# Products of full height in the attention and the HGRN heads of a hybrid trunk

## The chip, the cores and the metric

One Trainium2 chip, one core of it. The metric is the device time of one execution in microseconds (us); lower is better. The program is compiled once, and its times are the medians of several executions.

## What is computed

A trunk of two layers over L = 1024 + 16 positions, the first 16 being learned meta tokens. Layer 0 mixes with four HGRN heads and four attention heads side by side, layer 1 with trailing-mean pooling, and each layer ends in a squared-ReLU MLP. The change touches layer 0's mixers. Cut to that:

```python
def step(S, inp):                               # HGRN, one chunk of 64 positions
    qi, ki, vi, gi = inp
    b = jnp.cumsum(gi, axis=2)
    o_inter = jnp.einsum('bhtk,bhkv->bhtv', qi * jnp.exp(b), S)
    dec = jnp.exp(jnp.where(tri, b[:, :, :, None, :] - b[:, :, None, :, :], -jnp.inf))
    att = jnp.einsum('bhtk,bhtsk,bhsk->bhts', qi, dec, ki)
    o_intra = jnp.einsum('bhts,bhsv->bhtv', att, vi)
    b_last = b[:, :, -1:, :]
    S_new = jnp.exp(b_last[:, :, 0, :])[..., None] * S + jnp.einsum(
        'bhsk,bhsv->bhkv', ki * jnp.exp(b_last - b), vi)
    return S_new, o_inter + o_intra

def mla_mixer(...):                             # attention; a head's key: 128 own columns, 64 rope columns
    q, k = rope_tail(rmsnorm(q, qn_g), cos, sin), rope_tail(rmsnorm(k, kn_g), cos, sin)
    return block_causal_attention(q, k, v, cid)

def one_block(args):                            # 128 queries of one head, all keys
    s = jnp.einsum('bqhd,bkhd->bhqk', qblk, k) * scale
    mask = cid[None, :] <= qc[:, None]          # cid: 0 for the meta tokens, then one per 64 positions
    p = jax.nn.softmax(jnp.where(mask, s, -jnp.inf), axis=-1)
    return jnp.einsum('bhqk,bkhd->bqhd', p, v)
```

## The kernel before

Everything is float32. Where precision matters, a number is held as a high part (rounded to fp32r, a shorter float that TensorE multiplies in one pass) and a low part (the rest), and a product is three fp32r products: high by high, high by low, low by high (`mm3`, lines 156 to 158). Products of plain float32 appear in the trace as two records each. The program is one straight stream of instructions: the writer gives the order of the work, a scheduler with its own time model then sets the order on each engine, and the tile pools add the waits. So each edit can move its neighbours.

The stages, in order of time: `entry` and the first projections (to 100 us of the span); `hgrn_head` for four heads, in which the next projections fill in, then `mla_in` (100 to 355); `attention` (355 to 586); `out_proj` (586 to 680); then two MLPs with the pooling between them (680 to the end).

`attention` computes values for two heads (`values`, line 692), prepares keys and queries of a head (`head_prep`), and runs `qtile` for nine blocks of queries of each head, i = 7 down to -1. Block i has 128 queries (i = -1: the 16 meta tokens) and nk = 16 + 128 (i + 1) keys. The next head's preparation, and at the end the first products of `out_proj`, are interleaved by the scheduler. In `qtile`:

- **Scores** (line 774): the keys are cut into one to three pieces of at most 512, and each piece is a chain of five products into one bank `sc`. The fourth takes the query's rope part `qs` (high in rows 0 to 63, low in 64 to 127) against the high rope keys `ks[0]`, doubled over 128 rows; the fifth takes the high rows of `qs` alone against 64 rows of the low rope keys `ks[1]`. There are 60 chains.
- **Softmax**: DVE scales the scores and finds the maximum (778), ACT takes the exponential (783), DVE the reciprocal (785), DVE scales `p` (786). `p` has two buffers, `sc` has two banks.
- **Weighted values**: blocks of `p` are transposed on PE by a product with the identity (797), up to four to a bank `tp`; they are copied to `pts` (16 rows of meta keys on DVE, 800; the rest by an engine that the scheduler picks, 803) and multiplied with the values (806): `vm` holds those of the 16 meta tokens in rows 0 to 15, `va` those of 128 keys. There are 180 transposes and 180 value products, 36 of them with `vm`.

In `hgrn_head` the first chunk is the 16 meta tokens, and its products have 16 rows: the state from them (567, `kt` by `vm`) and their own output (583, `attM` by `vm`), each once a head. The notation `16*128` in the trace is the rows and columns of the weights that a product loads, and PEld is that load.

Of the kernel before, what the change touches and what calls it, by code (L numbers as in the profile page):

```python
# [17 lines left out]
P = 128  # L18
D = 1024
NM = 16  # L20
# [39 lines left out]
class Trunk:  # L60
# [336 lines left out]
    def mixer_in(self):  # L397
        nc, V = self.nc, self.nc.vector
        small = self.small(2, "att")
        self.att = small[:, :288].rearrange("p (c t) -> p c t", t=32)  # L400
        self.attM = small[:, 288:288 + P]
        self.attT = self.slot(13, "attT")[:, :8 * P].rearrange("p (c t) -> p c t", t=P)
        V.memset(self.attT, 0.0)
        V.memset(self.attM, 0.0)
        self.vm = self.mix.tile([P, 256], F32, name="vm", tag="vm")
        self.ms = [self.small(i, f"x{i}")[:, :BW] for i in range(2)]
        gs = [self.hgrn_head(j) for j in range(H)]
        self.mla_in()
        for j in range(H):
            for off, n in SPL0:  # L410
                s = slice(off, off + n)
                self.split(gs[j][:, s], self.uh[j][:, s], self.ul[j][:, s], V if j < 3 else nc.gpsimd)

    def hgrn_head(self, j):
        nc = self.nc
        TT, V = nc.vector.tensor_tensor, nc.vector
        f, k, q, v = (self.first[i // 2] if j == 0 and i % 2 == 0 else self.slot(4 * (j % 2) + i, x)
                      for i, x in enumerate("fkqv"))
        g = self.slot(8 + j, "g")
        v = v[:, :8 * P].rearrange("p (c v) -> p c v", v=P)  # L420
        vm = self.vm[:, (j % 2) * P:(j % 2 + 1) * P]
# [33 lines left out]
        for i, (off, n) in enumerate(SPL0):  # L455
# [7 lines left out]
            b = 0  # L463
            if i == 0:
                nc.tensor.transpose(pv3[:NM, 3], vt[:, :NM], self.ident)
                V.tensor_copy(out=vm[:NM], in_=pv3[:NM, 3])
                b = NM
            m = (n - b) // P
            for c in range(m):
                nc.tensor.transpose(pv3[:, c], vt[:, b + c * P:b + (c + 1) * P], self.ident)  # L470
            c0 = (off + b - NM) // P
# [32 lines left out]
        while n < P:  # L504
            base = 0 if n < NM else NM
            width = L - base
            if n <= 16:
                level(1 + n.bit_length() - 1, k, qa)
                if n == 16:
                    for r in range(4):  # L510
                        nc.scalar.copy(out=attT[32 * r:32 * r + 32, :, 32 * r:32 * r + 32],
                                       in_=att[32 * r:32 * r + 32, 1:])
            else:
                ps = self.bank("tp")
                ps3 = ps.rearrange("p (c t) -> p c t", t=64)
                for c in range(8):
                    for b in range(64 // n):
# [3 lines left out]
                                         start=True, stop=True, tile_position=(0, r))  # L521
# [25 lines left out]
        kt = f[:, :8 * P].rearrange("p (c v) -> p c v", v=P)  # L547
        for c0 in (0, 4):
            pk = self.bank("sc")
            pk3 = pk.rearrange("p (c v) -> p c v", v=P)  # L550
# [11 lines left out]
        for c0 in (0, 4):  # L562
            pk = self.bank("sc")
            pk3 = pk.rearrange("p (c v) -> p c v", v=P)
            for c in range(c0, c0 + 4):
                rows = NM if c == 0 else P
                nc.tensor.matmul(pk3[:, c - c0], kt[:rows, c], v[:, c - 1] if c else vm[:NM], start=True, stop=True)
            for c in range(c0, c0 + 4):
                s = k[:, c * P:(c + 1) * P]
                if c == 0:  # L570
                    V.tensor_copy(out=s, in_=pk3[:, 0])
                else:
                    V.scalar_tensor_tensor(out=s, in0=st[-1], scalar=dec[:, c - 1:c], in1=pk3[:, c - c0],
                                           op0=ALU.mult, op1=ALU.add)
                st.append(s)

        V.tensor_copy(out=self.attM[:NM, :NM], in_=att[:NM, 0, :NM])
        for b in range(3):
            po = self.bank("tp")[:, :BW].rearrange("p (c v) -> p c v", v=P)
            for i in range(3):  # L580
                c = 3 * b + i
                if c == 0:
                    nc.tensor.matmul(po[:, 0], self.attM[:NM], vm[:NM], start=True, stop=True)
                    continue
                nc.tensor.matmul(po[:, i], attT[:, c - 1], v[:, c - 1], start=True, stop=False)
                nc.tensor.matmul(po[:, i], qa[:, NM + P * (c - 1):NM + P * c], st[c], start=False, stop=True)
            sq = self.tmp()
            nc.scalar.activation(out=sq, in_=po, func=AF.Square)
            col = self.mix.tile([P, 4], F32, name="colh", tag="colh", bufs=3)
            V.tensor_reduce(out=col[:, :3], in_=sq.rearrange("p (c v) -> p c v", v=P), axis=AX.X, op=ALU.add)  # L590
            nc.scalar.activation(out=col[:, :3], in_=col[:, :3], func=AF.Sqrt, scale=1.0 / P, bias=self.eps)
            V.reciprocal(out=col[:, :3], in_=col[:, :3])
            on = self.tmp().rearrange("p (c v) -> p c v", v=P)
            TT(out=on, in0=po, in1=col[:, :3].unsqueeze(2).to_broadcast([P, 3, P]), op=ALU.mult)
            pt = self.bank("tp")
            for i in range(3):
                nc.tensor.transpose(pt[:, i * P:(i + 1) * P], on[:, i], self.ident)
            pieces = [(0, 0, NM), (P, NM, 2 * P)] if b == 0 else [(0, NM + P * (3 * b - 1), BW)]
            for c0, t, n in pieces:
                V.scalar_tensor_tensor(out=g[:, t:t + n], in0=pt[:, c0:c0 + n], scalar=self.col(C_HGN),  # L600
                                       in1=g[:, t:t + n], op0=ALU.mult, op1=ALU.mult)
# [53 lines left out]
    def attention(self):  # L655
        nc = self.nc
        row = lambda i, name: self.slot(i, name, F32R)

        kna = [row(2, "kna0"), row(3, "kna1")]
        self.v = [self.slot(i, "va")[:, :8 * P].rearrange("p (c v) -> p c v", v=P) for i in (8, 9)]  # L660
        self.vm = self.mix.tile([P, 256], F32, name="vm", tag="vm")
        self.npt = 0
        qna = [row(10, "qna0"), row(12, "qna1")]
        self.rrs = [self.slot(i, "rr") for i in (13, 7)]
        qs = [row(4, "qs0"), row(11, "qs1")]
        self.pb = [self.slot(i, "p") for i in (6, 5)]
        u6, u7 = ([self.uh[c], self.ul[c]] for c in (6, 7))

        qnb = [z[:, 0] for z in self.ckv]
        sets = [(kna, qna, qs[0]), (u7, u6, qs[1]), (kna, qna, qs[0]), (u7, qnb, qs[1])]  # L670
        self.values(0)
        hs = [self.head_prep(0, *sets[0]), self.head_prep(1, *sets[1])]
        for h in range(H):
            for i in reversed(range(-1, 8)):
                self.qtile(h, i, *sets[h], hs[h])
            if h == 1:
                self.values(1)
            if h + 2 < H:
                hs.append(self.head_prep(h + 2, *sets[h + 2]))
# [79 lines left out]
    def qtile(self, h, i, kn, qn, qs, rr):  # L759
        nc, V = self.nc, self.nc.vector  # L760
        t, rows, nk = (0, NM, NM) if i < 0 else (NM + P * i, P, NM + P * (i + 1))
        q = slice(t, t + P)
# [4 lines left out]
        for z in range(np_):  # L767
            a, b = z * step, min(nk, (z + 1) * step)
            ps = self.bank("sc")[:, :b - a]
            ks = slice(a, b)  # L770
            ops = [(qn[0][:, q], kn[0][:, ks]), (qn[0][:, q], kn[1][:, ks]), (qn[1][:, q], kn[0][:, ks]),
                   (qs[:, q], self.ks[0][:, ks]), (qs[:64, q], self.ks[1][:64, ks])]
            for m, (x, y) in enumerate(ops):
                nc.tensor.matmul(ps, x, y, start=(m == 0), stop=(m == 4))
            if b == nk and i >= 0:
                V.memset(ps[:64, b - a - 64:b - a], -1e30)

            V.tensor_tensor_reduce(out=p[:rows, a:b], in0=ps[:rows], in1=rr[0][:rows, ks], op0=ALU.mult, op1=ALU.max,
                                   scale=rr[1][:rows, 1 + i:2 + i],
                                   scalar=-3e38 if z == 0 else st[:rows, z - 1:z],  # L780
                                   accum_out=st[:rows, z:z + 1])
# [3 lines left out]
        V.reciprocal(out=st[:rows, 6:7], in_=st[:rows, 5:6])  # L785
        V.tensor_scalar(out=p[:rows, :nk], in0=p[:rows, :nk], scalar1=st[:rows, 6:7], scalar2=None, op0=ALU.mult)
        po = self.bank("tp")
        v, vm = self.v[h % 2], self.vm[:NM, (h % 2) * P:(h % 2 + 1) * P]
        last = i + 1
        for g0 in range(0, i + 2, 4):  # L790
            grp = range(g0, min(g0 + 4, i + 2))
            pt = self.bank("tp").rearrange("p (c q) -> p c q", q=P)
            sb = self.small(self.npt % 3, "pts").rearrange("p (c q) -> p c q", q=P)
            self.npt += 1
            for kt in grp:
                kr, k0 = (NM, 0) if kt == 0 else (P, NM + P * (kt - 1))
                nc.tensor.transpose(pt[:kr, kt - g0, :rows], p[:rows, k0:k0 + kr], self.ident[:rows, :rows])
            b = 0
            if g0 == 0:
                V.tensor_copy(out=sb[:NM, 0, :rows], in_=pt[:NM, 0, :rows])  # L800
                b = 1
            if len(grp) > b:
                nc.any.tensor_copy(out=sb[:, b:len(grp), :rows], in_=pt[:, b:len(grp), :rows])
            for kt in grp:
                kr = NM if kt == 0 else P
                nc.tensor.matmul(po[:, :rows], v[:, kt - 1] if kt else vm, sb[:kr, kt - g0, :rows],
                                 start=(kt == 0), stop=(kt == last))
        d = slice(t, t + rows)
        self.split(po[:, :rows], self.uh[4 + h][:, d], self.ul[4 + h][:, d])
# [555 lines left out]
```

## Time and profile before

| | us |
|---|---|
| median of 3 runs (2065.58 to 2076.06) | 2068.29 |
| profiled execution, its own time | 2067.88 |
| its span in the trace | 2066.1 |
| busy in the span: PE / PEld | 2002.0 / 1826.6 |
| busy in the span: DVE / POOL / ACT | 1441.1 / 887.7 / 880.0 |

A matmul's record has a modelled end, so the share of PE says little of its speed: the step from one product's start to the next one's is what counts. An idle stretch of an engine is put down to what ended it; "issue" is a wait for nothing that the profile shows.

### The profile page before, as it was taken

Reading aid. Unit: us, or ns where it says so; the run is one execution under the profiler, and the core shown is the slowest. Engines: PE = TensorE matmul, PEld = TensorE weight load, DVE = VectorE, ACT = ScalarE, POOL = GpSimd, SP = SyncE. Lnnn points to the kernel's source line nnn. Section 1 sums busy time; section 2 is a strip of 40 time slices with the busy share of each in tenths; the row PEclk is TensorE's granted clock in tenths of the full one; section 3 lists DMA queues with packets and bytes.
Section 4 is the critical chain, followed back from the end, with each engine's and each line's share of the span. In section 5 each row is a group of like instructions: output and inputs, shape, how many; then the busy total and the mean of one; then the engine's idle time right before and its main releaser. Section 6 shows DMA issues by size and latency. Waiting matters only on the chain. (4 is left out here: it accounts for less than half of the span.)

```text
span 2066.1 us, 37157 instructions
## 1 busy us (share of the span) xinstructions
PE 2002.0 (97%) x14440; PEld 1826.6 (88%) x14440; DVE 1441.1 (70%) x2385; ACT 880.0 (43%) x1800; POOL 887.7 (43%) x632
## 2 busy tenths in 40 slices
PE   8999999999999999999989999998999999999999
PEld 7999998888799999999989999997878887778887
DVE  7655557554454777767877767779787778888676
ACT  5232325554442544454623334466444445334331
POOL 6223223000021345454447777343454454488771
PEclk9999999999999899999999999998999999999999
DMA  4111100000031244443854340101444447653402
GB/s 149 42 33 32 42 27 30 13 11 11 27 114 32 93 139 155 152 143 140 265 179 156 121 135 19 57 26 67 148 143 143 153 147 254 211 168 128 138 21 102
DMA packets 114928, 215.20 MB, mean 104 GB/s; under 512 B 12224, under 2 KB 20672, under 8 KB 114752
## 3 DMA queue, kind: packets, MB, share of 16 engines
q1 hardware_dynamic: 114752, 212.83, 30.8%
q8 instruction: 113, 1.85, 0.4%
q14 instruction: 63, 0.52, 0.1%
HBM read 151.80 MB, written 60.99 MB: 103 GB/s over the span
## 5 line engine op out<-in xcount | busy, mean ns | idle before, releaser
L139 POOL TENSOR_TENSOR wl<-raw,wh 128x1024 fp32r<-128x1024 f32 x23 | 56.2, 2444 | 356.2 <-ACT wh L138 339.4
L138 ACT ACTIVATE A<-q 128x512 fp32r<-128x512 f32 x148 | 91.2, 621 | 213.7 <-PE sc L942 131.8
L139 POOL TENSOR_TENSOR A<-q,A 128x512 fp32r<-128x512 f32 x91 | 143.6, 1586 | 83.5 <-ACT A L138 55.9
L139 POOL TENSOR_TENSOR B<-q,B 128x512 fp32r<-128x512 f32 (+1 forms) x97 | 151.2, 1572 | 46.0 <-ACT B L138 46.0
L940 PE MATMUL tp<-B,A 128*128 128x260 f32 (+5 forms) x510 | 163.1, 320 | 7.2 <-DVE hT L1144 7.0
L156 PE MATMUL mm<-uh,wh 128*128 128x384 f32 (+1 forms) x504 | 165.1, 328 | 2.5 <-DVE z L450 2.5
L157 PE MATMUL mm<-ul,wh 128*128 128x384 f32 (+1 forms) x504 | 163.7, 325 | 0.0
L158 PE MATMUL mm<-uh,wl 128*128 128x384 f32 (+1 forms) x504 | 163.0, 324 | 0.4 <-DVE wl L139 0.4
L941 PE MATMUL tp<-B,A 128*128 128x260 f32 (+5 forms) x510 | 162.2, 318 | 0.5 <-DVE B L139 0.5
L942 PE MATMUL tp<-B,A 128*128 128x260 f32 (+5 forms) x510 | 161.6, 317 | 0.0
L139 POOL TENSOR_TENSOR r<-q,r 128x512 fp32r<-128x512 f32 x66 | 91.4, 1384 | 135.7 <-ACT r L138 135.7
L940 PE MATMUL mm<-B,A 128*128 128x260 f32 (+5 forms) x345 | 110.3, 320 | 3.5 <-ACT B L138 3.5
L940 PE MATMUL sc<-B,A 128*128 128x260 f32 (+5 forms) x345 | 110.0, 319 | 0.8 <-DVE hT L1144 0.7
L138 ACT ACTIVATE r<-q 128x512 fp32r<-128x512 f32 x131 | 81.8, 627 | 66.9 <-DVE q L985 36.5
L941 PE MATMUL mm<-B,A 128*128 128x260 f32 (+5 forms) x345 | 110.2, 319 | 0.0
L940 PEld LDWEIGHTS tp<-B,A 128*128 128x128 f32 x510 | 96.7, 190 | 15.0 <-DVE hT L1144 7.7
L942 PE MATMUL mm<-B,A 128*128 128x260 f32 (+5 forms) x345 | 109.9, 318 | 0.0
L941 PE MATMUL sc<-B,A 128*128 128x260 f32 (+5 forms) x345 | 109.6, 318 | 0.0
L942 PE MATMUL sc<-B,A 128*128 128x260 f32 (+5 forms) x345 | 109.5, 317 | 0.0
L1017 ACT ACTIVATE q<-q 128x260 f32<-128x260 f32 (+2 forms) x128 | 61.5, 484 | 103.7 <-DVE q L1016 103.3
L138 ACT ACTIVATE B<-q 128x512 fp32r<-128x512 f32 (+1 forms) x154 | 92.2, 620 | 27.4 <-PE sc L942 15.4
L941 PEld LDWEIGHTS tp<-B,A 128*128 128x128 f32 x510 | 96.5, 189 | 7.7 <-DVE B L139 0.7
(656 smaller groups left out, 7005.4 us busy)
## 6 DMA issues: line engine op xcount, KB each, us to landing
q<-in_w_dn_dram SPq DMA_DIRECT2D x88, 256.0 KB, 3.0
q<-in_w_up_dram SPq DMA_DIRECT2D x75, 256.0 KB, 2.6
q<-at SPq DMA_DIRECT2D x46, 256.0 KB, 3.3
q<-at SPq DMA_DIRECT2D x44, 260.0 KB, 3.8
raw<-in_w_in_dram SPq DMA_DIRECT2D x19, 512.0 KB, 3.5
q<-a SPq DMA_DIRECT2D x36, 256.0 KB, 3.6
a<-q SPq DMA_DIRECT2D x34, 260.0 KB, 2.9
a<-q SPq DMA_DIRECT2D x31, 256.0 KB, 2.9
```

The costliest lines, as they stand in the source:

```text
L138: self.nc.scalar.activation(out=hi, in_=src, func=AF.Copy)
L139: (eng or self.nc.vector).tensor_tensor(out=lo, in0=src, in1=hi.bitcast(F32), op=ALU.subtract)
L156: self.nc.tensor.matmul(out, wh, xh, start=(i == 0), stop=False)
L157: self.nc.tensor.matmul(out, wh, xl, start=False, stop=False)
L158: self.nc.tensor.matmul(out, wl, xh, start=False, stop=(i == n - 1))
L940: mm(ps, wh, xh, start=first and i == 0, stop=False, skip_group_check=True)
L941: mm(ps, wh, xl, start=False, stop=False, skip_group_check=True)
L942: mm(ps, wl, xh, start=False, stop=i == n - 1, skip_group_check=True)
L1017: nc.scalar.activation(out=dst[:, s], in_=dst[:, s], func=AF.Square)
```

## The change

Three edits, and the fourth that they need:

- The fifth score product takes all 128 rows of `qs` and of the low rope keys `ks[1]`. Those rows were there already (`sel` doubles the keys, and `split` works on all rows), so no instruction is added. It now also adds the query's low part by the low keys.
- All products with `vm` (HGRN 567 and 583, attention 806) take 128 rows. `vm` is set to zero first, by a MEMSET on DVE in `mixer_in` and one in `attention`; the rows of the other operand below the 16 hold old finite numbers.
- The transposes take 128 rows of `p` and 128 columns of it in each case; the first one, of the 16 meta keys, becomes one of keys 0 to 127, of which rows 16 and below meet zeros.
- With that, the copy of 16 rows is dropped, and one copy takes the whole bank.

```diff
@@ mixer_in
         self.vm = self.mix.tile([P, 256], F32, name="vm", tag="vm")
+        V.memset(self.vm, 0.0)
@@ hgrn_head
-                rows = NM if c == 0 else P
-                nc.tensor.matmul(pk3[:, c - c0], kt[:rows, c], v[:, c - 1] if c else vm[:NM], start=True, stop=True)
+                nc.tensor.matmul(pk3[:, c - c0], kt[:, c], v[:, c - 1] if c else vm, start=True, stop=True)
...
-                    nc.tensor.matmul(po[:, 0], self.attM[:NM], vm[:NM], start=True, stop=True)
+                    nc.tensor.matmul(po[:, 0], self.attM, vm, start=True, stop=True)
@@ attention
         self.vm = self.mix.tile([P, 256], F32, name="vm", tag="vm")
+        nc.vector.memset(self.vm, 0.0)
@@ qtile
             ops = [(qn[0][:, q], kn[0][:, ks]), (qn[0][:, q], kn[1][:, ks]), (qn[1][:, q], kn[0][:, ks]),
-                   (qs[:, q], self.ks[0][:, ks]), (qs[:64, q], self.ks[1][:64, ks])]
+                   (qs[:, q], self.ks[0][:, ks]), (qs[:, q], self.ks[1][:, ks])]
...
-        v, vm = self.v[h % 2], self.vm[:NM, (h % 2) * P:(h % 2 + 1) * P]
+        v, vm = self.v[h % 2], self.vm[:, (h % 2) * P:(h % 2 + 1) * P]
...
             for kt in grp:
-                kr, k0 = (NM, 0) if kt == 0 else (P, NM + P * (kt - 1))
-                nc.tensor.transpose(pt[:kr, kt - g0, :rows], p[:rows, k0:k0 + kr], self.ident[:rows, :rows])
-            b = 0
-            if g0 == 0:
-                V.tensor_copy(out=sb[:NM, 0, :rows], in_=pt[:NM, 0, :rows])
-                b = 1
-            if len(grp) > b:
-                nc.any.tensor_copy(out=sb[:, b:len(grp), :rows], in_=pt[:, b:len(grp), :rows])
+                k0 = NM + P * (kt - 1) if kt else 0
+                nc.tensor.transpose(pt[:, kt - g0], p[:, k0:k0 + P], self.ident)
+            nc.any.tensor_copy(out=sb[:, :m, :rows], in_=pt[:, :m, :rows])
             for kt in grp:
-                kr = NM if kt == 0 else P
-                nc.tensor.matmul(po[:, :rows], v[:, kt - 1] if kt else vm, sb[:kr, kt - g0, :rows],
+                nc.tensor.matmul(po[:, :rows], v[:, kt - 1] if kt else vm, sb[:, kt - g0, :rows],
                                  start=(kt == 0), stop=(kt == last))
```

The scheduler moves little outside attention: POOL's order is the same, two DMA stores change places with neighbours, and PE's order differs from row 1882 to row 2540 of 11649 and then at four places in the second MLP. Three places inside.

PE, head 1, first block (i = 7), where the first bank of transposes is followed by its value products. Before:

```order
L797 MATMUL tp<-cst,p 16x128
L797 MATMUL tp<-cst,p 128x128 x3
L806 MATMUL tp<-pts,vm 128x128
L797 MATMUL tp<-cst,p 128x128 x4
L806 MATMUL tp<-pts,va 128x128 x3
L797 MATMUL tp<-cst,p 128x128
L774 MATMUL sc<-uh 128x328
L774 MATMUL sc<-ul,uh 128x328
L774 MATMUL sc<-uh,ul 128x328
L774 MATMUL sc<-ks,qs_3928 128x328 x2
```

and now (lines are those of the changed kernel: 775 for 774, 800 for 797, 803 for 806):

```order
L800 MATMUL tp<-cst,p 128x128 x4
L775 MATMUL sc<-uh 128x328
L775 MATMUL sc<-ul,uh 128x328
L775 MATMUL sc<-uh,ul 128x328
L775 MATMUL sc<-ks,qs_3930 128x328 x2
L803 MATMUL tp<-pts,vm 128x128
L803 MATMUL tp<-pts,va 128x128 x3
L800 MATMUL tp<-cst,p 128x128 x5
```

The product with `vm` stood straight behind its transposes and now stands behind a whole score chain, and the other three value products follow it at once, without transposes between.

PE, head 3, the last blocks (i = 2 to -1), where the attention's work runs out and only a little of `out_proj` is between. Before:

```order
L797 MATMUL tp<-cst,p 128x128 x2
L806 MATMUL tp<-pts,vm 128x128
L156 MATMUL mm<-uh,wh 128x384
L806 MATMUL tp<-pts,va 128x128 x2
L157 MATMUL mm<-ul,wh 128x384
L158 MATMUL mm<-uh,wl 128x384
L797 MATMUL tp<-cst,p 16x128
L797 MATMUL tp<-cst,p 128x128
L806 MATMUL tp<-pts,vm 128x128
L797 MATMUL tp<-cst,p 16x16
L806 MATMUL tp<-pts,va 128x128
L806 MATMUL tp<-pts,vm 128x16
```

and now:

```order
L800 MATMUL tp<-cst,p 128x128 x3
L156 MATMUL mm<-uh,wh 128x384
L803 MATMUL tp<-pts,vm 128x128
L803 MATMUL tp<-pts,va 128x128 x2
L157 MATMUL mm<-ul,wh 128x384
L158 MATMUL mm<-uh,wl 128x384
L800 MATMUL tp<-cst,p 128x128 x2
L803 MATMUL tp<-pts,vm 128x128
L803 MATMUL tp<-pts,va 128x128
L800 MATMUL tp<-cst,p 128x128
L803 MATMUL tp<-pts,vm 128x16
```

One `out_proj` product moved ahead of a `vm` product, and the last transpose no longer stands between the last value products.

DVE, the end of the HGRN heads (the copies of head 3's keys `f`, line 561, before the query's scaling, 630), now:

```order
L558 COPY f<-sc 16x128
L559 COPY f<-sc 128x384
L561 COPY f<-sc 128x512
L662 MEMSET vm 128x256
L630 SCALAR_TENSOR_TENSOR z<-z,par,ss 128x384
```

The MEMSET is the new row; the four others stood there in this order before.

## Rows read from the trace of the kernel before

**Rows 1.** The page, part 1: busy us, share of the span, instructions.

```profile
PE 2002.0 (97%) x14440; PEld 1826.6 (88%) x14440; DVE 1441.1 (70%) x2385; ACT 880.0 (43%) x1800; POOL 887.7 (43%) x632
```

**Rows 2.** Busy time by stretch; after the engines PEclk, DMA share, GB/s.

```profile
355.00:586.00 231.00, 224.55 (x1426) 188.22 (x1425) 122.57 (x430) 114.24 (x285) 4.40 (x3) 1.00 0.09 29
...
680.00:693.00 13.00, 12.65 (x61) 12.56 (x60) 8.80 (x18) 5.45 (x11) 0.00 (x0) 0.51 0.12 42
```

**Rows 3.** PE's waits in 355 to 586: us in total, times, longest.

```profile
PE tp L806 <- DVE pts L800: 1.6, 4, 0.4
...
PE tp L806 <- ACT pts L803: 0.2, 1, 0.2
```

**Rows 4.** Weight loads, 355 to 586: busy us, mean ns, idle before.

```profile
L797 PEld LDWEIGHTS tp<-cst,p 128*128 128x128 f32 x144 | 17.5, 142 | 1.5
...
L774 PEld LDWEIGHTS sc<-ks,qs 128*128 128x128 f32 x60 | 11.3, 188 | 0.3 <-issue 0.2
L774 PEld LDWEIGHTS sc<-ks,qs 64*128 64x128 f32 x60 | 11.0, 183 | 11.6 <-issue 9.4
L806 PEld LDWEIGHTS tp<-pts,vm 16*128 16x128 f32 x72 | 10.5, 182 | 6.9 <-DVE pts L800 2.7 <-issue 1.5 <-DVE st L785 0.3
```

**Rows 5.** PE in order of time, a score chain: start us, us, instruction.

```profile
487.07 0.89 PE L774 MATMUL sc<-kna,qna 128*128 128x456 f32 x3
...
488.49 0.39 PE L692 MATMUL mm<-wh,ckv 128*128 128x256 f32 x1
488.72 0.28 PE L692 MATMUL mm<-wl,ckv 128*128 128x256 f32 x1
...
489.07 0.28 PE L692 MATMUL mm<-wl,ckv 128*128 128x256 f32 x1
```

**Rows 6.** PE in order of time, a product with vm.

```profile
482.60 0.39 PE L797 MATMUL tp<-cst,p 128*16 128x128 f32 x2
482.82 0.61 PE L806 MATMUL tp<-pts,va 128*128 128x128 f32 x4
483.36 0.48 PE L806 MATMUL tp<-pts,vm 16*128 16x128 f32 x2
483.78 0.49 PE L806 MATMUL tp<-pts,va 128*128 128x128 f32 x2
```

**Rows 7.** PE in order of time, what follows a product with vm.

```profile
432.96 0.94 PE L806 MATMUL tp<-pts,va 128*128 128x128 f32 x6
433.73 0.38 PE L797 MATMUL tp<-cst,p 128*16 128x128 f32 x2
```

**Rows 8.** PE in order of time, a product with vm in HGRN.

```profile
111.51 0.48 PE L583 MATMUL tp<-vm,att 16*128 16x128 f32 x2
111.93 0.39 PE L156 MATMUL mm<-uh,wh 128*128 128x272 f32 x1
112.16 0.29 PE L157 MATMUL mm<-ul,wh 128*128 128x272 f32 x1
```

**Rows 9.** Copies to pts on ACT in 355 to 586.

```profile
L803 ACT COPY pts<-tp 128x384 f32<-128x384 f32 x26 | 12.2, 472 | 10.5 <-PE tp L797 5.5 <-DVE pts L800 2.9 <-DVE st L782 1.8
...
L803 ACT COPY pts<-tp 128x512 f32<-128x512 f32 x7 | 4.1, 587 | 9.2 <-PE tp L797 9.2
```

**Rows 10.** Copies to pts on DVE in 355 to 586.

```profile
L800 DVE COPY pts<-tp 16x128 f32<-16x128 f32 x32 | 8.8, 275 | 9.5 <-PE tp L797 9.5
```

**Rows 11.** PE in order of time, head 3's last blocks.

```profile
580.64 0.49 PE L797 MATMUL tp<-cst,p 128*16 128x128 f32 x3
581.57 0.48 PE L806 MATMUL tp<-pts,vm 16*128 16x128 f32 x2 [0.44 <-DVE pts L800]
```

**Rows 12.** DVE in order of time, where the second MEMSET goes.

```profile
339.07 0.67 DVE L560 COPY f<-sc 128x512 f32<-128x512 f32 x1
340.73 0.62 DVE L630 SCALAR_TENSOR_TENSOR z<-z,par,ss 128x384 f32<-128x384 f32 x1 [0.99 <-ACT ss L185]
```

**Rows 13.** PE in the same place.

```profile
340.52 1.83 PE L567 MATMUL sc<-v,f 128*128 128x128 f32 x14
```

More of the change, by code (lines that the diff above doesn't have):

```diff
@@ L791, in qtile @@
             grp = range(g0, min(g0 + 4, i + 2))
+            m = len(grp)
             pt = self.bank("tp").rearrange("p (c q) -> p c q", q=P)
```

## The prediction

> **What bounds the kernel now.** First the busy line of the page: PE is busy for 97% of the span, DVE for 70%, ACT for 43% [rows 1]. Since a product's end is modelled, that says only that PE rarely stands still, not that it is quick. Then the stretch that the change touches most, attention from 355 to 586 us: PE 224.6 of 231 us at the full granted clock, DVE 122.6, ACT 114.2 [rows 2]. PE's waits on other engines there are seven rows, from 1.6 us down to 0.2, some 6 us in all [rows 3]. So in attention a microsecond off PE's own sequence is a microsecond off the end, as long as DVE and ACT, busy about half the time, deliver early enough.
>
> Third, PE's own sequence. The reader is to look at the idle time ahead of the weight loads: the same tile `qs` is loaded 60 times at 128 rows with 0.3 us of idle time ahead of all of them, and 60 times at 64 rows with 11.6 us, most of it put down to "issue", that is to no other engine [rows 4]. The loads of `vm` have 6.9 us ahead of 72, the transposes 1.5 us ahead of 144 [rows 4]. So something happens where the height of a product changes. Its full price stands in the steps from one start to the next.
>
> **The full-height step.** From 488.72 to 489.07 three fp32r products of 256 columns start, 0.117 us each [rows 5]; 256 columns at 2.4 GHz are 0.107, so a step is the columns plus 0.01. A weight load takes 0.19 [rows 4], longer than the step: at full height it is hidden behind the product ahead. Plain float32 records of 128 columns step by 0.11 (two from 482.60 to 482.82) [rows 6].
>
> A rule speaks against this. The Trainium skill, page "TensorE: Matmul & The Clock Gate", Part 3 (row/col tiling), says that a weight load overlaps products in flight only when its row group differs. By it a fifth product of full height would still load after the fourth, and the sum below would be near zero. The steps of 0.117 under loads of 0.19 [rows 4, 5] disagree with it for full height.
>
> **The change part by part.**
>
> The score chains. A chain of five products of 456 columns begins at 487.07, the next work at 488.49: 1.42 us. At full height it would be 5 x 0.20 = 1.00. The product behind the chain then steps by 0.23 (488.49 to 488.72) in place of 0.117, because its load came late as well: another 0.11. The chain's own first product has the same 0.11 from the switch ahead of it, which is in the 1.42 and belongs to that one. So one chain costs 0.42 - 0.11 + 0.11 = 0.42 too much [rows 5]; I take 0.40, as the step's extra of 0.01 is rounded. 52 of the 60 chains have 264 columns or more: 20.8 us. The eight of 144 and 16 columns are bound by their loads anyway, and I put 0.3 on them: 2.4. Together **23 us**. The lower bound is the idle time alone, 11.6 - 0.3 = 11.3 [rows 4]; I take the steps, since they hold the late loads too, which no idle row counts. The rows added to the fifth product cost nothing: its 128 rows stand in SBUF, and a load takes 183 ns at 64 rows and 188 at 128 [rows 4].
>
> The products with `vm` in attention. The two records take 0.42 (483.36 to 483.78) against 0.22: 0.20. The four ahead take 0.54 (482.82 to 483.36) against 0.44: 0.10 [rows 6]. The six behind take 0.77 (432.96 to 433.73) against 0.66: 0.11 [rows 7]. That is 0.4 where `vm` stands among value products, and 0.2 where it follows a score chain, whose exit already counts the rest. In the order before, 15 of the 36 follow a chain: 21 x 0.4 + 15 x 0.2 = **11 us**. Lower bound: 6.9 us of idle time, less the 2.7 + 0.3 put down to DVE [rows 4], 3.9.
>
> The eight products with `vm` in HGRN. 0.42 (111.51 to 111.93) against 0.22, and the product behind, of 272 columns, 0.23 against 0.123 [rows 8]: 8 x 0.31 = **2.5 us**, at least 1.
>
> The transposes. Two from 482.60 to 482.82 step by 0.11 although the first loads 16 columns [rows 6], so the height of the output is no switch, and full ones gain or lose nothing. The four for the meta tokens' queries grow from 16 columns to 128, at most 0.1 us each.
>
> The copies. DVE loses 36 copies, 32 of them 275 ns long [rows 10]. It was busy half the time: nothing, beyond a little slack. In return 24 copies on ACT grow from 384 to 512 columns, 472 to 587 ns [rows 9]: 2.8 us on an engine that was busy half the time. But now the first product of a bank, with `vm`, waits for the big copy instead of the small one. From the last transpose's step to its first product 0.28 (record; two end 0.39 after the first starts) - 0.11 + 0.59 + some 0.05, about 0.8 us, have to be covered [rows 6, 9]. I went through the new order of PE and laid the full-height steps on the work between: of the 60 banks, 50 have 0.8 us or more of other work there, and the missing pieces of the other ten add up to 4.7 us. Most lie at the ends of heads 1 and 3, as in the second order piece above. There PE waits already now, 0.44 us at 581.57 [rows 11], and the same count on the old order gives 6.5 us, of which the trace shows 1.6 + 0.2 as waits for copies [rows 3]: the switches were the cover for the rest. This cover goes. **I give back 3 us**; bounds 0 and 9.
>
> The MEMSETs. The first stands at the start, where DVE waits for parameters. The second is a new wait: `vm` has one buffer, so DVE stands until PE has read head 3's `vm` (the product before 340.52, whose result is out at about 340.6 [rows 13]), with the scaling at line 630 queued behind it. But that scaling starts only at 340.73, after 0.99 us of idle time [rows 12], so it is late by 0.2 to 0.3 us, and PE has value products to do meanwhile. Nothing; 0.3 us without that cover.
>
> **The sum.** 23 + 11 + 2.5 = 36.5, say 37 with HGRN's entries; less 3: 34 us. On the profiled execution, 2067.9 (span 2066.1 and 1.8 around it): 2033.9. That execution lies 0.4 under the median of the runs: **2034**. By the lower bounds, 11.3 + 3.9 + 1, the gain is 16.
>
> What is late next? Behind attention, `out_proj` and the MLPs keep their order, so the gain should pass through. A loose piece is the clock: from 680 to 693 us PE ran at 0.51 of its clock, the level of 1.2 GHz [rows 2], which costs 6.4 us, and where such stretches fall can change when everything moves by 34 us: 6 us either way.
>
> **The rivals.**
>
> *Half the gain (0.10).* The idle time goes, the late loads stay, or the softmax chain sets the pace in the last blocks of each head, where PE's cover is thin [rows 11]. For it: the switches were cover there, and PE waited in spite of them. Against it: DVE and ACT at half load [rows 2]. Gain 16: 2052.
>
> *The height is not the cause (0.05).* The idle time comes with the last place in a chain, or a full-height load behind a full-height product queues as well, and each of the 60 + 44 places costs what it did. Against it: `qs` as the fourth product has no idle time ahead of its load, and going over to `vm` from value products of the same kind costs 0.10 in the middle of an accumulation [rows 4, 6]. No gain, and the clock as it was: 2068. The Trainium skill's rule on row groups, above, would lead here.
>
> *Slower (0.05).* The big copy is on the path at each of the 60 banks, because ACT, which also runs the exponentials, comes to it late. If the new work between is no cover, 60 x 0.8 = 48 us are lost against 37 won, and 2079 results; it decides from 0.62 us a bank on. Against it: in the old order the copies of 384 had the same path, and PE waited 0.2 us for them in all [rows 3].
>
> **How the numbers follow.** The full gain has 0.80. Its own range is 2034 with 0 to 9 given back and 6 of clock: 2026 to 2046. To hold 8 in 10 it reaches slightly to the half gain: 2025 to 2048. A measurement of this kernel can tell about 0.5%, 10 us, from no change; so faster is 0.80 + 0.10 = 0.90, same 0.05, slower 0.05.
>
> **What would show it.** In the profile after, the idle time ahead of the fifth product's load should fall from 11.6 to below 1 us, five products of 456 columns should step by 0.20 each, the product behind them too, and two records of `vm` should take 0.22. The attention stretch should shrink from 231 to about 200 us, with 4 to 9 us of PE's waits in it, mostly for `pts` by ACT, at the ends of heads 1 and 3. If the stretch shrinks by half of that and PE's waits grow to 20 us, the half case holds; if idle time stays ahead of a load of 128 rows, the height was not the cause. The prediction is wrong in size above all if the late loads are not due to the switch.

## The result, and the profile after

The changed kernel takes **2039.9 us** (median of four runs, 2039.06 to 2041.79) against 2066.9 (2064.99 to 2076.06) for the kernel before on the same chip. The ratio is 0.9862, with a 95% interval of [0.9844, 0.9879]; ratios here go by all runs and not by the medians, so they differ slightly from the quotient of the two. The profiled executions have spans of 2039.0 and 2066.1, so 27.1 us are to be found in the traces. Lines move with the change: the score products are now at 775, the transposes at 800, their copy at 801, the value products at 803.

The page after, part 1, against [rows 1]. PE has as many instructions as before and is busy for the same 97%; DVE lost 36 copies. The page's shares don't show that anything happened.

```profile
PE 1974.5 (97%) x14440; PEld 1824.8 (89%) x14440; DVE 1435.6 (70%) x2349; ACT 883.4 (43%) x1806; POOL 885.9 (43%) x632
```

The attention stretch after, from 355 to 557 us, against [rows 2] (columns as there). It is 202 us long where it was 231, with the same kind of filling. The second row is new: for part of 366 to 380 us the granted clock was at its lower level, 1.2 GHz, which the kernel before did not show in attention.

```profile
355.00:557.00 202.00, 195.37 (x1406) 185.55 (x1407) 114.86 (x390) 115.31 (x286) 3.41 (x2) 0.98 0.09 29
366.00:380.00 14.00, 12.73 (x66) 12.06 (x65) 6.76 (x15) 6.34 (x15) 0.00 (x0) 0.76 0.07 20
```

The weight loads after, 355 to 557 us, against [rows 4] (busy us, mean ns, idle time before):

```profile
L800 PEld LDWEIGHTS tp<-cst,p 128*128 128x128 f32 x180 | 21.4, 142 | 1.2 <-PE mm L158 0.8 <-PE tp L803 0.2
L775 PEld LDWEIGHTS sc<-ks,qs 128*128 128x128 f32 x120 | 20.6, 189 | 0.3
...
L803 PEld LDWEIGHTS tp<-pts,vm 128*128 128x128 f32 x72 | 11.5, 189 | 3.8 <-ACT pts L801 3.4
```

`qs` is now loaded 120 times at 128 rows, and all of them together have 0.3 us of idle time ahead. The 60 loads of 64 rows had 11.6. What is left ahead of `vm` is a wait for the copy on ACT; "issue" is gone.

PE in order of time, the same place as [rows 5], one block of queries in head 2:

```profile
473.27 0.78 PE L775 MATMUL sc<-kna,qna 128*128 128x456 f32 x3
473.89 0.57 PE L775 MATMUL sc<-ks,qs 128*128 128x456 f32 x2
474.30 0.28 PE L693 MATMUL mm<-wh,ckv 128*128 128x256 f32 x1
474.42 0.28 PE L693 MATMUL mm<-wl,ckv 128*128 128x256 f32 x1
```

The chain takes 1.03 us (473.27 to 474.30) instead of 1.42, and the step behind it is 0.12 instead of 0.23. Around a `vm` product, against [rows 6, 7]:

```profile
408.29 0.38 PE L803 MATMUL tp<-pts,vm 128*128 128x128 f32 x2
408.51 0.83 PE L803 MATMUL tp<-pts,va 128*128 128x128 f32 x6
409.18 0.49 PE L800 MATMUL tp<-cst,p 128*128 128x128 f32 x3
```

Its two records take 0.22 (0.42 before) and the six behind 0.67 (0.77).

**An account of PE's steps.** The rows above are samples, so I went through every step from one product's start to the next one's, from the first score product to the last value product. A full-height step is put at the columns by 2.4 GHz plus 0.015 us, at least 0.112; what a step takes beyond that is sorted by where it stands. "Change of height" is a step into or out of a product of under 128 rows, or the one just behind; "waits" are steps over 0.25 us late; "low clock" is lateness of steps begun while the granted clock was at 1.2 GHz; "other" is the rest. A small delay beside a short product counts as "change of height", whatever its cause. Both kernels have 1364 steps there, and the full-height steps add up to 178.0 us in both. In us:

| | first score product at | attention | full height | change of height | other | waits | low clock | attention's end to the span's end |
|---|---|---|---|---|---|---|---|---|
| before | 364.7 | 220.5 | 178.0 | 31.6 | 3.4 | 7.5 | 0 | 1481.0 |
| after | 361.1 | 195.5 | 178.0 | 0 | 6.0 | 8.6 | 2.9 | 1482.4 |
| difference | -3.6 | -25.0 | 0 | -31.6 | +2.6 | +1.1 | +2.9 | +1.4 |

So 31.6 us came off, 6.6 came back inside attention, 3.6 were won ahead of it and 1.4 lost behind it. Counted in the same stretch, the kernel before has 83 separate runs of short products, so that one costs 0.38 us; the changed kernel has none.

### The profile page after: what moved, and what is told of

Read it like the earlier page. It is cut to its first block, busy times and chain, and to the rows that moved or that the text cites. A ratio compares the mean times of both kernels' runs of the same rounds, so it can differ in the third digit from the quotient of the medians.

```text
span 2039.0 us, 37138 instructions
## 1 busy us (share of the span) xinstructions
PE 1974.5 (97%) x14440; PEld 1824.8 (89%) x14440; DVE 1435.6 (70%) x2349; ACT 883.4 (43%) x1806; POOL 885.9 (43%) x632
## 5 line engine op out<-in xcount | busy, mean ns | idle before, releaser
L138 ACT ACTIVATE B<-q 128x512 fp32r<-128x512 f32 (+1 forms) x154 | 92.2, 620 | 27.1 <-PE sc L939 15.4
```

Of the source, the lines that this page charges most:

```text
L138: self.nc.scalar.activation(out=hi, in_=src, func=AF.Copy)
```

## The experiments

My theory: each place where a product of fewer than 128 rows stands among full ones costs PE some 0.4 us, and the change takes these places away. The main rival: the place in the chain, or the copies and the order, did it. The account above was made for each run; where only a size is told below, it is from the same columns.

### One part alone

The fifth score product of full height, everything else as before:

```diff
-                   (qs[:, q], self.ks[0][:, ks]), (qs[:64, q], self.ks[1][:64, ks])]
+                   (qs[:, q], self.ks[0][:, ks]), (qs[:, q], self.ks[1][:, ks])]
```

> The kernel before with one edit: the fifth score product of full height; vm, transposes and copies as before. Theory (each change of height costs PE about 0.2 us going in and out together with the late load behind it, 0.4 a chain): 60 chains give about 22 us, so about 2045 against 2067, and no idle time ahead of the fifth load. Rival (the copies and transposes brought most of the 27 us): under 5 us, 2062 or more.

Measured: 2054.7 us, ratio 0.9930 [0.9909, 0.9951]. That is 10 us above the forecast. In its trace 19.4 us of changes of height came off, and 6.2 us of low clock, 1.4 of waits and 0.9 of other delays came back.

The `vm` products of attention alone, with what they need:

```diff
+        nc.vector.memset(self.vm, 0.0)
...
-        v, vm = self.v[h % 2], self.vm[:NM, (h % 2) * P:(h % 2 + 1) * P]
+        v, vm = self.v[h % 2], self.vm[:, (h % 2) * P:(h % 2 + 1) * P]
...
+                k0 = NM + P * (kt - 1) if kt else 0
+                nc.tensor.transpose(pt[:, kt - g0], p[:, k0:k0 + P], self.ident)
+            nc.any.tensor_copy(out=sb[:, :m, :rows], in_=pt[:, :m, :rows])
...
-                nc.tensor.matmul(po[:, :rows], v[:, kt - 1] if kt else vm, sb[:kr, kt - g0, :rows],
+                nc.tensor.matmul(po[:, :rows], v[:, kt - 1] if kt else vm, sb[:, kt - g0, :rows],
```

> The kernel before with only the attention's vm edits: MEMSET, vm products of 128 rows, full transposes, one copy a bank; fifth score product at 64 rows, HGRN as before. Theory: 36 vm products at 0.2 to 0.4 us, about 11 us less 2 for waits on the larger copy: about 2058. Rival (larger copy on the path at most banks): no gain or a loss, 2067 or more.

Measured: 2058.9 us, 0.9951 [0.9936, 0.9966].

The HGRN products alone (the first MEMSET, and 567 and 583 with all rows):

```diff
+        V.memset(self.vm, 0.0)
...
+                nc.tensor.matmul(pk3[:, c - c0], kt[:, c], v[:, c - 1] if c else vm, start=True, stop=True)
...
+                    nc.tensor.matmul(po[:, 0], self.attM, vm, start=True, stop=True)
```

> The kernel before with only HGRN's edits: the first MEMSET and the eight products with vm at 128 rows. Theory: about 3 us, 2064, read in the trace as the time at which the attention's first score chain starts (364.6 us before) coming about 3 us earlier. Rival (the entry to attention moved for another reason): no change of that time.

Measured: 2068.55 us, 0.9994 [0.9982, 1.0007], so the forecast 3 us are not seen in the time.

The weight loads in attention, of the first and then of the second of these kernels (columns as above):

```profile
L774 PEld LDWEIGHTS sc<-ks,qs 128*128 128x128 f32 x120 | 20.8, 193 | 0.3
...
L806 PEld LDWEIGHTS tp<-pts,vm 16*128 16x128 f32 x72 | 10.5, 182 | 7.6 <-DVE pts L800 2.8 <-issue 2.0 <-DVE ul L139 0.5
```

```profile
L803 PEld LDWEIGHTS tp<-pts,vm 128*128 128x128 f32 x72 | 11.0, 189 | 5.1 <-ACT pts L801 2.8 <-issue 1.9 <-ACT p L784 0.2
L775 PEld LDWEIGHTS sc<-ks,qs 64*128 64x128 f32 x60 | 11.0, 183 | 12.0 <-issue 10.3
```

Each edit clears its own loads and leaves the other's as they were (7.6 against 6.9 for `vm`, 12.0 against 11.6 for the 64 rows). In the account, the first leaves 12.2 us of changes of height, so 19.4 came off; the second leaves 22.1, so 9.5 came off. Together that is 28.9, and both at once take 31.6: the missing 2.7 lie where a `vm` product follows a chain directly, so that neither edit alone makes PE's passage there one of full height. By the times, the three parts give 14.5 + 10.1 + 1.2 = 26 us (2071.36, the kernel before on that chip, by one less each ratio) against 28.5 for the whole (2066.93 in the same way), a difference well within the intervals.

In HGRN the new product is as quick as forecast, the product behind it is not. PE in order of time, the HGRN kernel, against [rows 8]:

```profile
111.57 0.49 PE L583 MATMUL tp<-vm,att 128*128 128x128 f32 x2
111.81 0.37 PE L156 MATMUL mm<-uh,wh 128*128 128x272 f32 x1
112.03 0.29 PE L157 MATMUL mm<-ul,wh 128*128 128x272 f32 x1
```

The two records take 0.24 instead of 0.42. But the step behind is still 0.22 where I had counted on 0.123. So such a place gave 0.18 us, not 0.31. The first score product starts 2.1 us earlier (362.6 against 364.7), of which eight such places are 1.4; the time's interval includes no change at all.

### Place, number and dose

The 64-row product in the second place of the chain instead of the last:

```diff
+            ops = [(qn[0][:, q], kn[0][:, ks]), (qs[:64, q], self.ks[1][:64, ks]), (qn[0][:, q], kn[1][:, ks]),
+                   (qn[1][:, q], kn[0][:, ks]), (qs[:, q], self.ks[0][:, ks])]
```

> The kernel before with the score chain's 64-row product moved from fifth to second place; same products, same result. Theory (the change of height costs, wherever it is): the same two changes a chain, time within 5 us of the kernel before, and the same 11 us of idle time ahead of the 60 loads of 64 rows. Rival (the last place in the chain costs): the idle time goes, about 2050.

Measured: 2074.28 us, 1.0018 [1.0007, 1.0029].

The fourth product with 64 rows as well, beside the fifth:

```diff
-                   (qs[:, q], self.ks[0][:, ks]), (qs[:64, q], self.ks[1][:64, ks])]
+                   (qs[:64, q], self.ks[0][:64, ks]), (qs[:64, q], self.ks[1][:64, ks])]
```

> The kernel before with the fourth score product cut to 64 rows too (it leaves out the query's low rope part), so that each chain has two products of 64 rows side by side. Theory (it is the change that costs, not the low product): one change in and one out as before, so the same time within 5 us, and next to no idle time ahead of the second of the two loads. Rival (each product of 64 rows costs): about 20 us more, 2087.

Measured: 2074.44 us, 1.0017 [0.9997, 1.0038].

The 64-row product twice, in the second place and in the last, with full products between:

```diff
+            ops = [(qn[0][:, q], kn[0][:, ks]), (qs[:64, q], self.ks[1][:64, ks]), (qn[0][:, q], kn[1][:, ks]),
+                   (qn[1][:, q], kn[0][:, ks]), (qs[:, q], self.ks[0][:, ks]), (qs[:64, q], self.ks[1][:64, ks])]
```

> The kernel before with a second copy of the 64-row product at second place of each score chain, so that each chain changes height four times instead of twice (the low rope keys are added twice, which the reference does not do). Theory: 60 more products, 19008 columns at 2.4 GHz, 8 us plus 1 of steps, and 60 more pairs of changes at the 0.32 us that undoing the chains alone showed, 19: about 28 us more, 2095. Rival (a fixed price a chain, or the queue hides a second change): 9 us more, 2076.

Measured: 2112.5 us, 1.0194 [1.0155, 1.0234].

The loads of `qs` in these three, in that order:

```profile
L774 PEld LDWEIGHTS sc<-ks,qs 128*128 128x128 f32 x60 | 11.3, 189 | 0.2
L774 PEld LDWEIGHTS sc<-ks,qs 64*128 64x128 f32 x60 | 11.0, 183 | 10.4 <-issue 8.8
```

```profile
L774 PEld LDWEIGHTS sc<-ks,qs 64*128 64x128 f32 x120 | 18.2, 189 | 11.9 <-issue 9.8
```

```profile
L774 PEld LDWEIGHTS sc<-ks,qs 64*128 64x128 f32 x120 | 22.3, 186 | 22.2 <-issue 18.1
...
L774 PEld LDWEIGHTS sc<-ks,qs 128*128 128x128 f32 x60 | 11.5, 192 | 0.4 <-issue 0.3
```

The idle time goes with the 64 rows and not with the place: 10.4 us in the second place, while the load that is now last, of 128 rows, has 0.2. With two products of 64 rows side by side there are 120 such loads and still 11.9 us, as with 60. With two apart there are 22.2. So a passage into another height and out again is what costs, and a second product of the same height in it is free. The account says the same in full size: the changes of height are 31.1 us with two side by side (31.6 before), and 53.8 with two apart, 22.2 more for 60 more passages, or 0.37 us each. In the second place they are 36.8, 5.2 more: 14 `vm` products that stood directly behind the chain's 64-row product now stand apart from it, which makes 97 runs of short products out of 83.

The kernel with two apart was 43 us slower where 28 had been forecast. The passages (22.2) and the 60 added products (9.3) explain 31.5. What is over is clock: the stretch as a whole, and the longest part of it at the lower level (columns as in the windows above).

```profile
355.00:630.00 275.00, 270.29 (x1480) 213.60 (x1479) 123.92 (x431) 115.09 (x285) 4.38 (x3) 0.94 0.09 27
363.00:384.00 21.00, 20.53 (x78) 16.69 (x77) 5.88 (x11) 5.56 (x12) 1.00 (x1) 0.60 0.00 0
```

The granted clock is 0.94 in the mean; as it is either full or half, that is 2 x 0.06 x 275, some 33 us at 1.2 GHz, and the account puts 17.2 us of lateness down to it. In the 21 us of the second row PE was busy for 20.5 with 78 products, where the whole stretch has 113 in as long a time: busy by the records, slow by the clock.

### The copies

The transposes of full size and the one copy a bank, the `vm` products still with 16 rows:

```diff
+                k0 = NM + P * (kt - 1) if kt else 0
+                nc.tensor.transpose(pt[:, kt - g0], p[:, k0:k0 + P], self.ident)
+            nc.any.tensor_copy(out=sb[:, :m, :rows], in_=pt[:, :m, :rows])
```

> The kernel before with the full transposes and the one copy a bank, but the vm products (16 rows) and the score products (64 rows) as before. Theory: transposes and copies bring nothing by themselves, 2064 to 2071, and the larger copy adds at most 3 us of PE's waits. Rival (they are part of the gain): 2060 or less.

Measured: 2067.85 us, 0.9992 [0.9977, 1.0007]. Copies and transposes alone do nothing, and the changes of height stay at 31.3 us.

The changed kernel with two copies for the first bank of each block: its first 128 columns by DVE, the rest by an engine that the scheduler picks. It ran twice, the second time beside the changed kernel itself:

```diff
+            z = 0
+            if g0 == 0:
+                V.tensor_copy(out=sb[:, 0, :rows], in_=pt[:, 0, :rows])
+                z = 1
+            if m > z:
+                nc.any.tensor_copy(out=sb[:, z:m, :rows], in_=pt[:, z:m, :rows])
```

> The changed kernel with the copy of a first bank in two again: DVE copies the 128 columns of the first key block (128 rows), the other engine the rest. Theory (the larger copy costs at most the few us of waits at the ends of heads 1 and 3): within 3 us of the changed kernel, 2037 to 2043. Rival (the one copy is what ate 7 us of the forecast gain): about 2034, with PE's waits for pts gone.

Measured: 2037.57 us, 0.9845 [0.9826, 0.9864].

> e4 again beside the changed kernel on one chip. Theory (the one copy is not what took the missing gain, and e4's profile had PE waits of the same size and no fall of the clock in attention): within 3 us of the changed kernel's run here. Rival (the second copy on DVE is the better form): 2 us or more faster than it, with an interval that leaves equality out.

Measured: 2042.13 us, 0.9866 [0.9842, 0.9889].

> The changed kernel again. Theory: 2040 as before; in the attention stretch 195 us, of which the falls of the clock are 0 to 7 us and differ from execution to execution, since the step accounts of the other runs show falls in some and none in others. Rival (the change itself brings the falls of the clock): 3 us or more of them here too, at the same places, 366 and 376 us.

Measured: 2039.84 us (2035.61 to 2045.9), 0.9857 [0.9827, 0.9888]. In its trace attention takes 194.3 us, with 8.9 us of waits, 5.7 of other delays and 1.8 of low clock, which fell twice in this window (columns as above):

```profile
358.00:381.00 23.00, 21.74 (x131) 20.65 (x131) 10.33 (x22) 9.41 (x21) 1.00 (x1) 0.85 0.04 12
```

So the account repeats to some 0.3 us but for the clock. The rival's 3 us of low clock are not reached, though one of the two falls came again at 376 us.

One copy or two is the same within these intervals. PE's waits in attention for the copies, of the changed kernel and then of the first run with two (us in total, times, longest):

```profile
PE tp L803 <- ACT pts L801: 1.9, 5, 0.5
```

```profile
PE tp L808 <- DVE pts L803: 1.6, 4, 0.5
...
PE tp L808 <- ACT pts L806: 1.2, 3, 0.6
```

1.9 us against 1.6 + 1.2: the earlier small copy brings nothing. No version here beats the changed kernel by more than the runs differ among themselves.

### The ends of the heads

At the end of head 3 PE waits for ACT; the changed kernel, PE in order of time:

```profile
550.87 0.49 PE L803 MATMUL tp<-pts,vm 128*128 128x128 f32 x2 [0.27 <-ACT pts L801]
...
555.28 0.49 PE L803 MATMUL tp<-pts,vm 128*128 128x128 f32 x2 [0.52 <-ACT pts L801]
...
556.42 0.40 PE L803 MATMUL tp<-pts,vm 128*128 128x16 f32 x2 [0.32 <-ACT pts L801]
```

To take these waits away, I changed the order of the blocks in the kernel with two copies, so that small and large blocks alternate, in all heads and then in heads 1 and 3 only (the two buffers of `p` are taken in turn by the new order, which the cut below leaves out):

```diff
-            for i in reversed(range(-1, 8)):
+            for n, i in enumerate((7, -1, 6, 0, 5, 1, 4, 2, 3)):
```

> The changed kernel with two copies a first bank and the query blocks of each head in the order 7, -1, 6, 0, 5, 1, 4, 2, 3, so that small blocks stand between large ones. Theory (what is left in attention is PE waiting at the ends of heads 1 and 3, about 9 us in steps that are over 0.25 us late, where only small blocks are left to cover the copies): 2 to 5 us less than e4b, 2033 to 2036. Rival (those waits come from the softmax chain and move with the blocks): same as e4b or slower.

Measured: 2063.1 us, 0.9963 [0.9948, 0.9978].

> As e9, but the mixed order in heads 1 and 3 alone. Theory: the same gain as e9, since heads 0 and 2 have other work as cover. Rival: no gain over e4b.

Measured: 2060.38 us, 0.9959 [0.9942, 0.9975].

Neither tells anything about the tail. Head 3 writes its output over its own keys, which the descending order can do, since a block's keys end where its queries do. In the mixed order later blocks of head 3 read what was overwritten, so that head computes something else, and its scores wait for that output (the third row below). PE's waits of the first of the two, in 355 to 583 us:

```profile
PE tp L800 <- DVE p L787: 5.5, 3, 3.9
PE tp L800 <- DVE st L786: 5.2, 3, 2.5
...
PE sc L775 <- ACT uh L138: 1.4, 4, 0.4
```

In the account waits rose from 9.9 us (two copies, blocks descending) to 23.7, and 10.4 us of low clock came on top; how much of this the overwriting causes is not shown. Whether the ends of the heads can be filled stays open; an order that keeps head 3's blocks descending was not tried.

## Why the prediction was right, and where its sizes were off

The forecast was 2034 with 2025 to 2048; the time came out at 2039.9, and the mechanism was the one named. Some of the sizes were off, and one came out by luck. By its steps:

- **The score chains: 23 forecast, 22.1 measured** (31.6 less the 9.5 that `vm` alone takes off). Taking the steps and not the idle time (11.3, the lower bound) was right: the late load behind the change is as real as the idle time ahead of it. Had I stopped at the idle rows, half of the gain would have been missed. The half-gain rival falls with the steps of 0.12 behind the chain.
- **`vm` in attention: 11 forecast, 9.5 measured.** The discount where `vm` follows a chain, 15 x 0.2 = 3, is the 2.7 that the two single edits leave over.
- **HGRN: 2.5 forecast, 2.1 earlier by the HGRN edit alone**, 1.4 of it from the eight places. What was mis-sized is the late product behind, 0.22 still: it belongs to the products of 64 columns ahead (see the last section). Attention of the changed kernel begins 3.6 us earlier; 1.7 of that is a fall of the clock at 218 us in the kernel before (its window of 216 to 224 us below), which the changed one did not have, and 1.9 is left.

```profile
216.00:224.00 8.00, 6.28 (x28) 6.28 (x29) 3.61 (x10) 5.80 (x10) 0.00 (x0) 0.79 0.00 0
```

- **The transposes and the MEMSETs: nothing forecast, nothing seen.** The 16-column transposes in the kernel with the score edit alone, and the full ones in the kernel with the copies alone, leave the account as it is.
- **The copies: 3 forecast as waits for `pts`, and these waits went only from 1.8 us [rows 3] to 1.9.** In the account waits and other small delays together rose by 3.7 (1.1 + 2.6), so the size was right by luck. I had said that the waits for `pts` at the ends of heads 1 and 3 would be most of 4 to 9 us. All waits in the profile add up to 7.3, of which the three at the end of head 3 are 1.1. The larger copy is not shown to be the cause: two copies in place of one give nothing back (9.9 us of waits and 6.4 of other delays), the kernel with the copies alone has no such rise (6.4 and 3.2), and the one with the score edit alone, which keeps the small copy, has part of it (8.9 and 4.3). Besides, 1.2 of the 2.6 stand ahead of `vm` products, where the account put any small delay under the height before, so they need not be new.
- **The clock: within its 6 us.** In attention 2.9 us, which the kernel before had none of. The two runs of one and the same kernel with two copies show how loose this is: 194.3 us of attention and no such stretch in one, 198.0 and 3.5 us of it in the other. The kernel before itself goes from 2065 to 2076 over its runs. So as far as these runs show, this is a spread of the runs and not a cost of the change; the kernel before has one trace only.
- **Behind attention 1.4 us** were lost, and that stretch lies between 1476.8 and 1487.5 over all kernels, with no edit in it.

34 forecast, 27.1 found: 0.9 + 1.5 less from chains and `vm`, 0.7 more given back, 2.9 + 1.4 for the clock and the rest, and 1.1 more ahead of attention than the 2.5, from the fall that didn't come. That leaves 0.6, of which 0.5 is the forecast's own step from 36.5 to 37.

**The rivals.** That the height is not the cause is refuted by the three kernels on place, number and dose: in attention idle time and late steps follow the passages between heights, not the place in the chain and not the number of short products. With it falls the rule of the Trainium skill, page "TensorE: Matmul & The Clock Gate", Part 3, as far as full height goes: it has a load overlap products in flight only if its row group differs. Here 120 loads of 128 rows behind products of 128 rows have 0.3 us of idle time, and products of 256 columns step by 0.12 under loads of 0.19. The Trainium skill, page "TensorEngine Tiling (Array Packing)", Key Properties, states that a change of tiling mode drains TensorE. The idle time at each passage fits that, if a product of 64 or 16 rows counts as another mode, which no run here shows. What the runs show is the price, some 0.37 us for the way in and out, shared by neighbours of the same height. The slower case, the big copy on the path at 60 banks, is refuted by the kernel with the copies alone.

## What to carry to other kernels

Where a few products of fewer rows stand among products of 128, count the changes of height, not the rows, and changes to fewer columns with them: fill the rows with zeros (or with rows that are there anyway) to full height, or put the short products side by side so that they share one passage. Read the price from the steps from start to start around such a product, the one behind it included, since the idle time ahead of the load shows about half. Then look for what the lost time had hidden: here 3.7 us of waits and small delays came back, not mainly on the copy that I had expected.

## What was not expected of the hardware

- The second of two adjacent 64-row products was free: 120 loads had 11.9 us of idle time where 60 had 11.6.
- A transpose that loads 16 columns (`128*16`) is no such change: it stepped by 0.11 like a full one [rows 6].
- Height is not all. Products of full height but fewer columns, in HGRN 16, 32 or 64, have such passages too, 32 times ahead of attention in the changed kernel. Its rows show it at a place without `vm`: the step into 32 columns is 0.26 where 384 columns otherwise step by 0.18, and the product behind steps by 0.28. So the 0.22 behind HGRN's full-height `vm` product reads as the exit from the 64 columns ahead of it. The transposes of 16 columns are the exception.

```profile
104.55 0.34 PE L158 MATMUL mm<-uh,wl 128*128 128x384 f32 x1
104.73 0.33 PE L156 MATMUL mm<-uh,wh 128*128 128x384 f32 x1
104.99 0.70 PE L521 MATMUL tp<-q,k 128*32 128x32 f32 x32
105.62 0.44 PE L157 MATMUL mm<-ul,wh 128*128 128x384 f32 x1
105.90 0.34 PE L158 MATMUL mm<-uh,wl 128*128 128x384 f32 x1
```

- 60 added passages came with some 33 us of attention at 1.2 GHz. Of the profiles with about as many passages as before, two had 13 to 14 us of it (HGRN alone, two of 64 rows side by side), one some 18 (copies alone) and two none (the kernel before, the second place). The score edit alone, with fewer than half of the passages, had some 13 too. So it is not shown that the passages cause it.
